# adaLN dots ordered behind the residual additions, second-GEMM weights requested two outputs ahead, norm tiles first, and mean squares of q and k token by token

## The chip, the core and the metric

The kernel is one program on one core of a Trainium2 chip. The metric is the device time of one execution in microseconds (us). Each version is timed by the median of several executions on the same chip; one more execution is recorded by the hardware profiler, and the profile and the trace come from that one. The engines have the names of the profile: PE (matmul; its weight loads are listed as PEld), DVE (vector), ACT (scalar and activation), POOL, and SP, which here only issues DMAs.

## What is computed

Two residual layers over x (512 tokens, 1024 features, fp32). Every layer modulates its norms by vectors computed from c:

```python
mod = silu(c) @ ada_w[layer] + ada_b[layer]          # 6 vectors of 1024
shift1, scale1, gate1, shift2, scale2, gate2 = split(mod)
h = rms_norm(x, norm_mix[layer]) * (1 + scale1) + shift1
y = mixer_conv_hgrn(h)          # layer 0
y = mixer_stick_breaking(h)     # layer 1: q, k = rms_norm of each head (64 wide), then attention
x = x + gate1 * y
h = rms_norm(x, norm_mlp[layer]) * (1 + scale2) + shift2
x = x + gate2 * (square(relu(h @ mlp_w1[layer])) @ mlp_w2[layer])   # 1024 -> 4096 -> 1024
```

## The kernel before

**Arithmetic.** Activations lie transposed: features on the 128 partitions, the 512 tokens along the free axis, in 8 tiles of features; tokens are often handled as two halves (hf 0 and 1) of 256. Every large matmul is done in three, with both operands split in a high and a low part: `mm3` issues whi x h_hi, whi x h_lo, wlo x h_hi (lines 281, 282, 283). A weight piece of 512 KB is loaded by SP into a raw buffer (`raw_w`; tile `wraw`, **3 buffers**, shared by both MLP matrices and the adaLN weights), cast to `whi` on ACT (L271) and reduced to `wlo` on DVE (L272), each with 4 buffers. The raw buffer is free for the next load when `wlo` is done.

**adaLN dots.** The modulation vectors are 1024-long dot products. `background(n)` takes the next n from a list: each loads a 512 KB piece of `ada_w` into a raw buffer and reduces it on DVE (`ada_dot`, L419; in the listings of order it is the row `ISA wraw,modr<-wraw,cb`, with a short second row `ISA modr`). 48 dots are spread over the four blocks of layer 0's MLP by the table `PIECES` (13, 13, 12 and 10 of them); in layer 1 the list is empty.

**The MLP** of layer 0 runs from about 264 to 604 us, that of layer 1 from 890 us to the end. It has a head (first norm half and four hidden tiles) and then four blocks b = 0 to 3. In each block a first GEMM makes hidden tiles in pairs (`pair`: seven 128x256 products from three sums of weights and activations, tiles `wa`, `wb`, `wc`, `wd`; `kept` copies one result to SBUF on ACT), the last step of which is deferred (`rest`), ending in a relu, square and split (`hidh`, `hidl` L291). The second GEMM then makes 8 outputs o (24 matmuls each, `products`): outputs 0 and 1 run their first seven eighths before and after `rest`, then both are finished, and o = 2 to 7 follow. `second(o)` asks for the weights w_o, `done(o)` adds the result to the residual (`x_add`, L505, tile `x`) and calls `background`. In block 3 `done` also squares x for the next norm (`nsq` on ACT L485, `nss` on DVE L490), only outputs 0 to 4 go this way, and 5, 6 and 7 follow in halves. While output 6 runs, `pair_w` asks for the weights of the next block's first pair.

**What sets the order.** PE's order in the MLPs is the order in which the code is written. DVE, ACT and SP are put in order in the MLP by the Tile scheduler, with priorities from the order of writing. The attention of layer 1 and both of its norms (the attention's, about 604 to 622 us, and the one before its MLP, about 884 to 898 us) are ordered by a planner (`on_pe`, `on_dve`, `on_act` give each operation's tiles, cost and a priority; lower goes first). Within an engine everything runs strictly in order.

**Two small places.** In `mlp_head` a timer `later(TN, ...)` with TN = 2.0 places the two matmuls with `ones` that finish the second half's norm (L496) after two of the eight k steps on PE. In attention, `mean_squares` sums the squares of q and k per head: a matmul with the 128x32 head selector `hs` (a slice of the tile `cons`) as the stationary operand and all the tokens moving (L1459), an ACT copy into `rows` (L1461), and one transpose per 128 tokens (L1465) to bring tokens onto partitions; DVE adds EPS (L1468).

Of the kernel before, what the change touches and what calls it, by code (L numbers as in the profile page):

```python
# [23 lines left out]
P = 128  # L24
T = 512
# [195 lines left out]
def trunk(tc, x_d, c_d, rep_d, small_d, const_d, ada_d, ws_d, win_d, wv_d, woab_d, w1_d, w2_d, wqk_d, wvc_d, woc_d, out_d):  # L221
# [130 lines left out]
    def acc():  # L352
        return mps.tile([P, T], F32, name="acc", tag="acc", bufs=4)
# [83 lines left out]
    def mcol(l, v, f):  # L437
        c = l * 48 + v * 8 + f
        return modc[:, c:c + 1]
# [62 lines left out]


    def x_add(o, ps, sl, l, v):
        dve.scalar_tensor_tensor(x[o][:, sl], ps, mcol(l, v, o), x[o][:, sl], op0=ALU.mult, op1=ALU.add)  # L505

# [174 lines left out]
    def later(delay, fn):  # L681
        count[0] += 1
        heapq.heappush(heap, (clk[0] + delay, count[0], fn))
# [458 lines left out]
    def mlp(l, last, hp, head, th, more=()):  # L1142

        nrm = Norm(1, 0, (7,)) if not last else None
        ahead = None
        for b in range(4):
            hid, rest = list(head) if b == 0 else [], lambda: None
            if b == 0:
                for n, j in enumerate((4, 5)):
                    whole_tile(more[n] if more else load_w(w1_d[l, j]), j, hp, hid)  # L1150
            for i in range(len(hid) // 2, 4):
                rest = pair(4 * b + i, hp, th, hid, rest, ahead or pair_w(l, 4 * b + i, hp))
                ahead = None
            n = 8 if b < 3 else 7 if last else 5
            second = lambda o: (acc(), load_w(w2_d[l, b // 2, o, b % 2], None, AT256 if o == n - 1 else AT512))

            def products(p, k0, k1):
                for k in range(k0, k1):
                    mm3(p[0], p[1], ks(k), hid[k], FULL, k == 0, k == 7)

            def done(o, ps):
                x_add(o, ps, FULL, l, GATE2)
                if b == 3:
                    if last:
                        sync.dma_start(out_d[o], x[o])
                    else:
                        nrm.add(o, FULL)
                if o < len(PIECES[b]):
                    background(PIECES[b][o])

            p0 = second(0)
            products(p0, 0, 7)
            rest()
            p1 = second(1)
            products(p1, 0, 7)
            for o, p in enumerate((p0, p1)):
                products(p, 7, 8)
                done(o, p[0])
            for o in range(2, n):
                p = p1 if o == n - 1 and b < 3 else second(o)  # L1180
                if o == n - 2 and b < 3:

                    p1, ahead = second(n - 1), pair_w(l, 4 * b + 4, hp)
                    next(ahead)
                    next(ahead)
                products(p, 0, 8)
                done(o, p[0])
                if o == n - 2 and b < 3:
                    w = next(ahead)
                    ahead = [w]  # L1190
# [109 lines left out]
    rows_ = in_ap([P, T], F32, "rows")  # L1300
# [99 lines left out]
    def finish(parts, hf, l, which, table, after=()):  # L1400
# [12 lines left out]
        for i in range(NT):  # L1413
            t_, g, sh = tth[i][hf], l * 16 + which * 8 + i, mcol(l, SHIFT1 if which == 0 else SHIFT2, i)
            hi, lo = hh[hf][i]

            on_dve(310, lambda i=i, t_=t_, g=g: dve.scalar_tensor_tensor(t_.t[:, sl], x[i][:, sl], gsc[:, g:g + 1], y.t,
                   op0=ALU.mult, op1=ALU.mult), (xh[i, hf], y), (t_,), -hf)
            on_act(256, lambda t_=t_, sh=sh, hi=hi: act.activation(hi.t[:, sl], t_.t[:, sl], AF.Identity, bias=sh), (t_,), (hi,), -hf,  # L1419
                   column=True)  # L1420
            on_dve(310, lambda t_=t_, sh=sh, hi=hi, lo=lo: dve.scalar_tensor_tensor(lo.t[:, sl], t_.t[:, sl], sh,  # L1421
                   hi.t[:, sl].bitcast(F32), op0=ALU.add, op1=ALU.subtract), (t_, hi), (lo,), -hf)


    QQ, KK, kraw, sqs, rq, oT, vs = {}, {}, {}, {}, {}, {}, {}
# [18 lines left out]
    def k_evict(p, ps, cut, sl):  # L1444
# [4 lines left out]
        on_act(n, lambda: act.copy(kraw[p].t[:, sl], cut(ps.t)), (ps,), (kraw[p],), 0, psum=True)  # L1449
        on_act(n, lambda: act.activation(sq.t[:, sl], cut(ps.t), AF.Square), (ps,), (sq,), 0, psum=True)  # L1450

    def mean_squares(p, bs, s0):

        if bs[0] == 0:
            rq[p] = [rrs[i].new() for i in range(4)]
        ms, row, col, m = miscs.new(), rows_.new(), miscs.new(), rq[p][0]
        sl, n = slice(P * bs[0], P * bs[-1] + P), P * len(bs)
        for s in range(2):
            on_pe(0.13, lambda s=s, sq=sqs[p, s, s0]: pe.matmul(ms.t[64 + 32 * s:96 + 32 * s, sl], hs, sq.t[:, sl], start=True, stop=True),  # L1459
                  (sqs[p, s, s0],), (ms,), 0)  # L1460
        on_act(n, lambda: act.copy(row.t[64:, sl], ms.t[64:, sl]), (ms,), (row,), 0, psum=True)  # L1461

        def flip():
            for b in bs:
                pe.transpose(col.t[:, 64 * b:64 * b + 64], row.t[64:, ks(b)], ident[64:, 64:])  # L1465
        on_pe(0.08 * len(bs), flip, (row,), (col,), 0)
        bb = slice(bs[0], bs[-1] + 1)
        on_dve(16, lambda: dve.tensor_scalar(  # L1468
            m.t.rearrange("p (s b h) -> p s b h", s=2, b=4)[:, :, bb],
            col.t[:, 0:256].rearrange("p (b s h r) -> p s b h r", b=4, s=2, h=2)[:, :, bb, :, 0], EPS, None, op0=ALU.add), (col,), (m,), 1)  # L1470

    def qk_norm(p):

# [332 lines left out]
```

## Time and profile before

| | before |
|---|---|
| median of 3 runs | 1236.03 us (1234.88 to 1237.93) |
| the profiled execution, its own time | 1238.95 us |
| its span | 1237.2 us, granted clock 0.997 |
| PE busy | 1213.8 us (98%) |
| DVE busy | 889.8 us (72%) |
| ACT busy | 618.5 us (50%) |
| DMA | 163.49 MB, mean 132 GB/s |

The profiled execution is 2.9 us above the median of the runs shown; 1.75 us of its time lie outside the span. An engine's busy time is a mean over very different stages. PE is the engine that is nearly always busy, so what moves the end is time in which PE waits, PE work added or removed, and stretches in which its granted clock is below 1.

### The profile page before, as it was taken

The page shows a single profiled execution, that of the slowest core. Times are in us where ns is not written, and L with a number is a line of the kernel's source. Part 1 is how long each engine was busy: PE and PEld are TensorE (multiplying, and loading weights), DVE is VectorE, ACT ScalarE, POOL GpSimd, SP SyncE. Part 2 cuts the span into 40 slices and gives each one's busy share as a digit, 9 for nine tenths or more (in the row PEclk, how much of TensorE's full clock was granted, in tenths as well). Part 3 has the DMA queues.
Part 4 walks back from the last instruction along what each step waited for, and adds up shares of the span by engine and source line. Part 5 has one row for each costly group of instructions (what it writes and reads, how often), then busy time and mean ns, then how long its engine had stood idle before and what let it go on. Part 6 is the DMA issues. An engine that isn't in the chain of part 4 may idle for free.

```text
span 1237.2 us, 19078 instructions
## 1 busy us (share of the span) xinstructions
PE 1213.8 (98%) x7601; PEld 1054.9 (85%) x7601; DVE 889.8 (72%) x1433; ACT 618.5 (50%) x1111; POOL 11.2 (1%) x24
## 2 busy tenths in 40 slices
PE   7999999999999999999999999999999999999998
PEld 6888877889799898898977778777898898998997
DVE  7996868779688787787867773669785585665752
ACT  4333232347257265274558754668464283472650
POOL 0000000000000000000200000000000000000000
PEclk9999999999999999999999999999999999999999
DMA  8765443623745726627432212322114223143141
GB/s 294 252 215 167 152 155 126 209 75 103 242 134 171 259 98 211 215 87 246 145 102 69 69 51 88 100 69 86 52 35 137 85 103 124 57 143 102 54 152 51
DMA packets 46329, 163.49 MB, mean 132 GB/s; under 512 B 5264, under 2 KB 5784, under 8 KB 46240
## 3 DMA queue, kind: packets, MB, share of 16 engines
q1 hardware_dynamic: 46096, 161.78, 39.4%
q8 instruction: 59, 0.97, 0.3%
q10 hardware_dynamic: 144, 0.49, 0.1%
q14 instruction: 30, 0.25, 0.1%
HBM read 155.96 MB, written 2.10 MB: 128 GB/s over the span
## 4 chain that ended last, share of the span: by engine, by line
PE 77%; DVE 10%; DMA 7%; ACT 4%; issue 2%; SPq 0%; ACTq 0%; DVEq 0%
PE b L281 19%; PE b L282 19%; PE b L283 19%; DMA wraw<-in_ada 2%; DMA raw<-in_ws 2%; DVE wlo L272 2%; PE acc L281 2%; PE acc L282 2%; PE acc L283 2%; PE b L1539 2%; PE b L1560 1%; DMA wraw<-in_w 1%; PE b L1595 1%; ACT whi L271 1%; PE b L1459 1%
## 5 line engine op out<-in xcount | busy, mean ns | idle before, releaser
L271 ACT CAST whi<-wraw 128x1024 fp32r<-128x1024 f32 x123 | 128.1, 1048 | 225.1 <-PE b L282 86.2
L282 PE MATMUL b<-hidl,whi 128*128 128x512 f32 (+1 forms) x544 | 205.8, 378 | 2.1 <-DVE hidl L291 2.1
L281 PE MATMUL b<-hidh,whi 128*128 128x512 f32 (+1 forms) x544 | 205.5, 378 | 0.0
L283 PE MATMUL b<-hidh,wlo 128*128 128x512 f32 (+1 forms) x544 | 205.1, 377 | 0.0
L281 PE MATMUL b<-hh,whi 128*128 128x256 f32 (+1 forms) x632 | 196.1, 310 | 1.5 <-ACT hh L1419 1.5
L282 PE MATMUL b<-hl,whi 128*128 128x256 f32 (+1 forms) x632 | 192.0, 304 | 0.7 <-DVE hl L1421 0.7
L283 PE MATMUL b<-hh,wlo 128*128 128x256 f32 (+1 forms) x632 | 192.0, 304 | 0.0
L272 DVE TENSOR_TENSOR wlo<-wraw,whi 128x1024 fp32r<-128x1024 f32 x123 | 150.0, 1223 | 57.1 <-ACT whi L271 55.6
L281 PEld LDWEIGHTS b<-hh,whi 128*128 128x128 f32 x632 | 119.6, 189 | 13.5 <-issue 7.2
L282 PEld LDWEIGHTS b<-hl,whi 128*128 128x128 f32 x632 | 120.7, 191 | 5.4 <-DVE hl L1421 1.1
L283 PEld LDWEIGHTS b<-hh,wlo 128*128 128x128 f32 x632 | 119.4, 189 | 5.3
L282 PEld LDWEIGHTS b<-hidl,whi 128*128 128x128 f32 x544 | 102.4, 188 | 22.3 <-DVE hidl L291 3.8
L505 DVE SCALAR_TENSOR_TENSOR x<-b,modc,x 128x512 f32<-128x512 f32 (+1 forms) x100 | 67.7, 684 | 74.4 <-PE b L283 74.2
L283 PEld LDWEIGHTS b<-hidh,wlo 128*128 128x128 f32 x544 | 102.2, 188 | 19.2 <-DVE wlo L272 0.2
L281 PEld LDWEIGHTS b<-hidh,whi 128*128 128x128 f32 x544 | 102.1, 188 | 18.7
L419 DVE CUSTOM_DVE_ANT_0 wraw<-wraw,cb 128x1024 f32<-128x1024 f32 x80 | 97.2, 1222 | 23.1 <-DMA wraw<-in_ada 22.8
L272 DVE TENSOR_TENSOR wlo<-tt,whi 128x1024 fp32r<-128x1024 f32 x52 | 63.4, 1221 | 26.0 <-ACT whi L271 25.4
L271 ACT CAST whi<-tt 128x1024 fp32r<-128x1024 f32 x52 | 53.4, 1050 | 42.5 <-PE b L282 27.7
L1372 DVE TENSOR_TENSOR wlo<-raw,whi 128x1024 fp32r<-128x1024 f32 x36 | 44.0, 1222 | 24.8 <-ACT whi L1371 24.6
L291 DVE TENSOR_TENSOR hidl<-cm,hidh 128x256 fp32r<-128x256 f32 (+1 forms) x90 | 44.6, 512 | 20.6 <-ACT hidh L290 19.5
L281 PE MATMUL acc<-hh,whi 128*128 128x512 f32 x128 | 52.2, 408 | 0.0
L1523 DVE TENSOR_TENSOR_SCAN om<-om,pat 128x772 f32<-128x772 f32 (+2 forms) x24 | 46.5, 1937 | 5.8 <-ACT om L1519 5.8
(378 smaller groups left out, 2634.5 us busy)
## 6 DMA issues: line engine op xcount, KB each, us to landing
wraw<-in_w SPq DMA_DIRECT2D x122, 512.0 KB, 4.0
wraw<-in_ada SPq DMA_DIRECT2D x80, 512.0 KB, 3.9
eraw<-in_ada SPq DMA_DIRECT2D x16, 512.0 KB, 3.7
wraw<-in_win SPq DMA_DIRECT2D x16, 512.0 KB, 3.4
raw<-in_wqk SPq DMA_DIRECT2D x16, 512.0 KB, 4.0
raw<-in_ws SPq DMA_DIRECT2D x8, 512.0 KB, 6.1
wraw<-in_woab SPq DMA_DIRECT2D x8, 512.0 KB, 3.2
raw<-in_wvc SPq DMA_DIRECT2D x8, 512.0 KB, 3.2
```

The costliest lines, as they stand in the source:

```text
L271: act.copy(hi, raw)
L272: dve.tensor_tensor(lo, raw, hi.bitcast(F32), op=ALU.subtract)
L281: pe.matmul(ps, whi, h[0][:, hs], start=start, stop=False, **kw)
L282: pe.matmul(ps, whi, h[1][:, hs], start=False, stop=False, **kw)
L283: pe.matmul(ps, wlo, h[0][:, hs], start=False, stop=stop, **kw)
L291: dve.tensor_tensor(lo[:, sl], t_[:, sl], hi[:, sl].bitcast(F32), op=ALU.subtract)
L419: dve.tensor_tensor_reduce(out=raw, in0=raw, in1=cb, scale=1.0, scalar=0.0, op0=ALU.mult, op1=ALU.add, accum_out=modr[:, col:col + 1])
L505: dve.scalar_tensor_tensor(x[o][:, sl], ps, mcol(l, v, o), x[o][:, sl], op0=ALU.mult, op1=ALU.add)
L1372: on_dve(1024, lambda: dve.tensor_tensor(lo.t, raw.t, hi.t.bitcast(F32), op=ALU.subtract), (raw, hi), (lo,), 1)
L1459: on_pe(0.13, lambda s=s, sq=sqs[p, s, s0]: pe.matmul(ms.t[64 + 32 * s:96 + 32 * s, sl], hs, sq.t[:, sl], start=True, stop=True), (sqs[p, ...
L1523: on_dve(2 * nw, lambda: dve.tensor_tensor_scan(s_(), s_(), pats[i][:, ::-1], 0.0, op0=ALU.mult, op1=ALU.max), (om,), (om,), 2)
L1539: pe.transpose(tp.t[:, o_:o_ + P], be.t[:, w0:w0 + P], ident)
```

## The change

Four edits.

1. In the MLP, `done(o)` now asks for the weights of output o + 2 itself, ahead of `background`, and the dots that `background` issues are tied behind the addition to x of that output by an ordering edge on DVE (`tc.issue_after`, no instruction and no semaphore). The loads of the dots are not tied.
2. In the head of layer 0's MLP the timer goes from TN to 2 TN.
3. In layer 1's norms the first three tiles of the first half get priority -1.
4. `mean_squares` takes the squares as the stationary operand, 128 tokens at a time, and two columns of `hs` as the moving one, so that tokens come out on partitions: 8 matmuls per call for 512 tokens, and neither ACT copy nor transposes; the tile `rows` is gone.

```diff
-            def done(o, ps):
-                x_add(o, ps, FULL, l, GATE2)
+            def done(o):
+                added = x_add(o, ps_[o][0], FULL, l, GATE2)
                 if b == 3:
                     if last:
                         sync.dma_start(out_d[o], x[o])
                     else:
                         nrm.add(o, FULL)
+                if o + 2 < n:
+                    ps_[o + 2] = second(o + 2)
                 if o < len(PIECES[b]):
-                    background(PIECES[b][o])
-            p0 = second(0)
-            products(p0, 0, 7)
+                    with tc.issue_after(added.ins):
+                        background(PIECES[b][o])
+            ps_ = {0: second(0)}
+            products(ps_[0], 0, 7)
             rest()
-            p1 = second(1)
-            products(p1, 0, 7)
-            for o, p in enumerate((p0, p1)):
-                products(p, 7, 8)
-                done(o, p[0])
+            ps_[1] = second(1)
+            products(ps_[1], 0, 7)
+            for o in range(2):
+                products(ps_[o], 7, 8)
+                done(o)
             for o in range(2, n):
-                p = p1 if o == n - 1 and b < 3 else second(o)
                 if o == n - 2 and b < 3:
-                    p1, ahead = second(n - 1), pair_w(l, 4 * b + 4, hp)
+                    ahead = pair_w(l, 4 * b + 4, hp)
...
     def mlp_head(l, nin, hp):
-        later(TN, lambda: nin.finish(acc(256), 1))
+        later(2 * TN, lambda: nin.finish(acc(256), 1))
...
+            first = -1 if hf or i < 3 else 0
             on_dve(310, lambda ...: ..., (xh[i, hf], y), (t_,), -hf)   # all three: -hf becomes first
...
+    hs2 = hs[:, 0:32:16]
     def mean_squares(p, bs, s0):
-        for s in range(2):
-            on_pe(0.13, lambda s=s, sq=sqs[p, s, s0]: pe.matmul(ms.t[64 + 32 * s:96 + 32 * s, sl], hs, sq.t[:, sl], start=True, stop=True),
-                  (sqs[p, s, s0],), (ms,), 0)
-        on_act(n, lambda: act.copy(row.t[64:, sl], ms.t[64:, sl]), (ms,), (row,), 0, psum=True)
-        def flip():
-            for b in bs:
-                pe.transpose(col.t[:, 64 * b:64 * b + 64], row.t[64:, ks(b)], ident[64:, 64:])
-        on_pe(0.08 * len(bs), flip, (row,), (col,), 0)
+        def sums_of():
+            for s in range(2):
+                for b in bs:
+                    pe.matmul(col.t[:, 8 * s + 2 * b:8 * s + 2 * b + 2], sq[s].t[:, ks(b)], hs2, start=True, stop=True)
+        on_pe(0.22 * len(bs), sums_of, sq, (col,), 0)
```

DVE at block 0's second GEMM, before. `wlo` is the split of a weight piece, `hidl` the split of a hidden tile that PE reads, x_61 and x_62 the residual tiles of outputs 0 and 1.

```order
L272 TENSOR_TENSOR wlo<-wraw,whi 128x1024
L291 TENSOR_TENSOR hidl<-cm,hidh 128x256
L419 ISA wraw,modr<-wraw,cb 128x1024
L419 ISA modr 128x1
L419 ISA wraw,modr<-wraw,cb 128x1024
L419 ISA modr 128x1
L419 ISA wraw,modr<-wraw,cb 128x1024
L419 ISA modr 128x1
L505 SCALAR_TENSOR_TENSOR x_61<-b_2826,modc,x_61 128x512
L505 SCALAR_TENSOR_TENSOR x_62<-b_2870,modc,x_62 128x512
L432 TENSOR_TENSOR gsc<-modr,adb 128x8
L272 TENSOR_TENSOR wlo<-wraw,whi 128x1024
```

Eight of the block's 13 dots stand ahead of the first two additions there, the last three of them in these rows. The same place in the changed kernel:

```order
L272 TENSOR_TENSOR wlo<-wraw,whi 128x1024
L291 TENSOR_TENSOR hidl<-cm,hidh 128x512
L291 TENSOR_TENSOR hidl<-cm,hidh 128x256 x2
L505 SCALAR_TENSOR_TENSOR x_61<-b_2826,modc,x_61 128x512
L505 SCALAR_TENSOR_TENSOR x_62<-b_2870,modc,x_62 128x512
L419 ISA wraw,modr<-wraw,cb 128x1024
L419 ISA modr 128x1
L419 ISA wraw,modr<-wraw,cb 128x1024
L419 ISA modr 128x1
L272 TENSOR_TENSOR wlo<-wraw,whi 128x1024
L505 SCALAR_TENSOR_TENSOR x_63<-b_2902,modc,x_63 128x512
```

The hidden tiles' splits have no dot among them any more, and all 13 dots of the block stand behind the addition of output 1 (x_62): a1 and a2, the split of w4, the addition of output 2, and then, further down, a3 a4 a5, x3, w5, a6 a7, x4, a8, w6, a9 a10, x5, a11, w7, a12 a13, x6, and only then the next pair's `wa` and sums. (a1 to a13 are the dots, x2 to x6 the additions, w4 to w7 the splits of those outputs' weights.) In blocks 1 and 2 it is the same, with 13 and 12 dots.

ACT at the end of block 3, before. Outputs 5, 6 and 7 use the last `whi` casts of `wraw`; `raw` holds weights of attention; x_65 is the residual tile of output 4, L339 an activation table load.

```order
L271 CAST whi<-wraw 128x1024
L485 ACTIVATE nsq<-x_63 128x512
L271 CAST whi<-wraw 128x1024 x2
L485 ACTIVATE nsq<-x_64 128x512
L271 CAST whi<-wraw 128x1024
L1371 CAST whi<-raw 128x1024 x2
L485 ACTIVATE nsq<-x_65 128x512
L339 ACT_TABLE_LOAD
```

And in the changed kernel:

```order
L485 ACTIVATE nsq<-x_64 128x512
L485 ACTIVATE nsq<-x_65 128x512
L339 ACT_TABLE_LOAD
L271 CAST whi<-wraw 128x1024 x3
L1372 CAST whi<-raw 128x1024 x3
```

The casts of w5, w6 and w7 stand behind the square of output 4 and behind the table load; SP likewise issues eight dot loads in a row ahead of w5, w6, w7.

DVE at the norm before layer 1's MLP, before (x_66 to x_68 are the last residual tiles of attention, `tt` the normed tiles of the first half, `hl` their low parts, which PE reads):

```order
L505 SCALAR_TENSOR_TENSOR x_65<-b_8687,modc,x_65 128x256
L505 SCALAR_TENSOR_TENSOR x_66<-b_8700,modc,x_66 128x256
L1395 TENSOR_TENSOR nss<-nss,nsq 128x256
L505 SCALAR_TENSOR_TENSOR x_67<-b_8713,modc,x_67 128x256
L1395 TENSOR_TENSOR nss<-nss,nsq 128x256
L505 SCALAR_TENSOR_TENSOR x_68<-b_8727,modc,x_68 128x256
L1417 SCALAR_TENSOR_TENSOR tt<-x_61,gsc,ny 128x256
```

And in the changed kernel:

```order
L505 SCALAR_TENSOR_TENSOR x_65<-b_8669,modc,x_65 128x256
L1419 SCALAR_TENSOR_TENSOR tt<-x_61,gsc,ny 128x256
L1419 SCALAR_TENSOR_TENSOR tt<-x_62,gsc,ny 128x256
L1419 SCALAR_TENSOR_TENSOR tt<-x_63,gsc,ny 128x256
L1396 TENSOR_TENSOR nss<-nss,nsq 128x256
L1423 SCALAR_TENSOR_TENSOR hl_8735<-tt,modc,hh_8723 128x256
```

Three normed tiles and their low parts now stand ahead of the last three additions of the other half. On PE the planner puts the whole of attention in another order as a result of edits 3 and 4; the two `ones` matmuls of edit 2 stand 24 matmuls later.

More of the change, by code (lines that the diff above doesn't have):

```diff
@@ L504, in x_add @@
     def x_add(o, ps, sl, l, v):
-        dve.scalar_tensor_tensor(x[o][:, sl], ps, mcol(l, v, o), x[o][:, sl], op0=ALU.mult, op1=ALU.add)
+        return dve.scalar_tensor_tensor(x[o][:, sl], ps, mcol(l, v, o), x[o][:, sl], op0=ALU.mult, op1=ALU.add)
     new_h()
@@ L1167, in done @@
                         nrm.add(o, FULL)
+                if o + 2 < n:
+                    ps_[o + 2] = second(o + 2)
                 if o < len(PIECES[b]):
-                    background(PIECES[b][o])
-            p0 = second(0)
-            products(p0, 0, 7)
+                    with tc.issue_after(added.ins):
+                        background(PIECES[b][o])
+            ps_ = {0: second(0)}
+            products(ps_[0], 0, 7)
             rest()
-            p1 = second(1)
-            products(p1, 0, 7)
-            for o, p in enumerate((p0, p1)):
-                products(p, 7, 8)
-                done(o, p[0])
+            ps_[1] = second(1)
[3 more added lines that the diff above has]
+                done(o)
             for o in range(2, n):
-                p = p1 if o == n - 1 and b < 3 else second(o)
                 if o == n - 2 and b < 3:
-                    p1, ahead = second(n - 1), pair_w(l, 4 * b + 4, hp)
+                    ahead = pair_w(l, 4 * b + 4, hp)
                     next(ahead)
                     next(ahead)
-                products(p, 0, 8)
-                done(o, p[0])
+                products(ps_[o], 0, 8)
+                done(o)
                 if o == n - 2 and b < 3:
-                    w = next(ahead)
-                    ahead = [w]
+                    ahead = [next(ahead)]
         if not last:
@@ L1299, in trunk @@
     vrs, oTs, krows = in_ap([P, 4, 256], F32, "v", 2), in_ap([P, T], F32R, "oT", 10), in_ap([4, T], F32R, "krow")
-    rows_ = in_ap([P, T], F32, "rows")
     rrs = [in_ap([P, 16], F32, f"r{i}", n) for i, n in enumerate((2, 1, 3, 3))]
@@ L1415, in finish @@
             hi, lo = hh[hf][i]
+            first = -1 if hf or i < 3 else 0
             on_dve(310, lambda i=i, t_=t_, g=g: dve.scalar_tensor_tensor(t_.t[:, sl], x[i][:, sl], gsc[:, g:g + 1], y.t,
-                   op0=ALU.mult, op1=ALU.mult), (xh[i, hf], y), (t_,), -hf)
-            on_act(256, lambda t_=t_, sh=sh, hi=hi: act.activation(hi.t[:, sl], t_.t[:, sl], AF.Identity, bias=sh), (t_,), (hi,), -hf,
+                   op0=ALU.mult, op1=ALU.mult), (xh[i, hf], y), (t_,), first)
+            on_act(256, lambda t_=t_, sh=sh, hi=hi: act.activation(hi.t[:, sl], t_.t[:, sl], AF.Identity, bias=sh), (t_,), (hi,), first,
                    column=True)
             on_dve(310, lambda t_=t_, sh=sh, hi=hi, lo=lo: dve.scalar_tensor_tensor(lo.t[:, sl], t_.t[:, sl], sh,
-                   hi.t[:, sl].bitcast(F32), op0=ALU.add, op1=ALU.subtract), (t_, hi), (lo,), -hf)
+                   hi.t[:, sl].bitcast(F32), op0=ALU.add, op1=ALU.subtract), (t_, hi), (lo,), first)
     QQ, KK, kraw, sqs, rq, oT, vs = {}, {}, {}, {}, {}, {}, {}
@@ L1455, in mean_squares @@
             rq[p] = [rrs[i].new() for i in range(4)]
-        ms, row, col, m = miscs.new(), rows_.new(), miscs.new(), rq[p][0]
-        sl, n = slice(P * bs[0], P * bs[-1] + P), P * len(bs)
-        for s in range(2):
-            on_pe(0.13, lambda s=s, sq=sqs[p, s, s0]: pe.matmul(ms.t[64 + 32 * s:96 + 32 * s, sl], hs, sq.t[:, sl], start=True, stop=True),
-                  (sqs[p, s, s0],), (ms,), 0)
-        on_act(n, lambda: act.copy(row.t[64:, sl], ms.t[64:, sl]), (ms,), (row,), 0, psum=True)
-        def flip():
-            for b in bs:
-                pe.transpose(col.t[:, 64 * b:64 * b + 64], row.t[64:, ks(b)], ident[64:, 64:])
-        on_pe(0.08 * len(bs), flip, (row,), (col,), 0)
+        col, m, sq = miscs.new(), rq[p][0], [sqs[p, s, s0] for s in range(2)]
+        view = lambda t_: t_.rearrange("p (s b h) -> p s b h", s=2, b=4)
+        def sums_of():
[3 more added lines that the diff above has]
+        on_pe(0.22 * len(bs), sums_of, sq, (col,), 0)
         bb = slice(bs[0], bs[-1] + 1)
-        on_dve(16, lambda: dve.tensor_scalar(
-            m.t.rearrange("p (s b h) -> p s b h", s=2, b=4)[:, :, bb],
-            col.t[:, 0:256].rearrange("p (b s h r) -> p s b h r", b=4, s=2, h=2)[:, :, bb, :, 0], EPS, None, op0=ALU.add), (col,), (m,), 1)
+        on_dve(16, lambda: dve.tensor_scalar(view(m.t)[:, :, bb], view(col.t[:, 0:16])[:, :, bb], EPS, None, op0=ALU.add), (col,), (m,), 1)
     def qk_norm(p):
```

## Prediction

> **What bounds the kernel now.** I read the engine totals and the chain first: they say which engine's time is the program's time.
>
> ```profile
> span 1237.2 us, 19078 instructions
> PE 1213.8 (98%) x7601; PEld 1054.9 (85%) x7601; DVE 889.8 (72%) x1433; ACT 618.5 (50%) x1111; POOL 11.2 (1%) x24
> PE 77%; DVE 10%; DMA 7%; ACT 4%; issue 2%; SPq 0%; ACTq 0%; DVEq 0%
> ```
>
> PE is busy in all but 23 us. So three things move the end: a PE wait removed, a PE wait added, and PE work. The waits of PE come next; the rows that the change touches are these.
>
> ```profile
> PE b L496 <- DVE nss L490: 2.4, 1, 2.4
> PE b L282 <- DVE hidl L291: 2.1, 4, 1.1
> PE b L281 <- ACT hh L1419: 1.5, 1, 1.5
> PE b L282 <- DVE hl L1421: 0.7, 1, 0.7
> ```
>
> All that the removal of waits can bring is 6.7 us. The third view is the timeline of DVE and PE over block 0's second GEMM, since the dots move there (start and length in us, engine, line, operation, tiles, and in brackets the idle time before it and what ended it).
>
> ```profile
> 313.83 1.23 DVE L419 CUSTOM_DVE_ANT_0 wraw<-wraw,cb 128x1024 f32<-128x1024 f32 x1 [1.73 <-DMA wraw<-in_ada]
> 314.98 1.02 DVE L291 TENSOR_TENSOR hidl<-cm,hidh 128x512 fp32r<-128x512 f32 x2
> ...
> 320.66 1.22 DVE L272 TENSOR_TENSOR wlo<-wraw,whi 128x1024 fp32r<-128x1024 f32 x1 [2.37 <-ACT whi L271]
> ...
> 322.17 1.22 DVE L419 CUSTOM_DVE_ANT_0 wraw<-wraw,cb 128x1024 f32<-128x1024 f32 x1
> 323.32 1.22 DVE L419 CUSTOM_DVE_ANT_0 wraw<-wraw,cb 128x1024 f32<-128x1024 f32 x1
> 325.25 1.22 DVE L419 CUSTOM_DVE_ANT_0 wraw<-wraw,cb 128x1024 f32<-128x1024 f32 x1 [0.71 <-DMA wraw<-in_ada]
> 326.41 1.41 DVE L505 SCALAR_TENSOR_TENSOR x<-b,modc,x 128x512 f32<-128x512 f32 x2
> 329.05 1.23 DVE L272 TENSOR_TENSOR wlo<-wraw,whi 128x1024 fp32r<-128x1024 f32 x1 [1.17 <-ACT whi L271]
> 337.39 1.23 DVE L272 TENSOR_TENSOR wlo<-wraw,whi 128x1024 fp32r<-128x1024 f32 x1 [2.44 <-ACT whi L271]
> 345.54 1.22 DVE L272 TENSOR_TENSOR wlo<-wraw,whi 128x1024 fp32r<-128x1024 f32 x1 [1.24 <-ACT whi L271]
> 349.08 0.69 DVE L1071 TENSOR_TENSOR tt<-wraw 128x512 f32<-128x512 f32 x1
> 351.05 0.40 PE L281 MATMUL b<-hidh,whi 128*128 128x512 f32 x1
> 356.65 0.28 PE L281 MATMUL b<-hh,whi 128*128 128x256 f32 x1
> 357.60 0.28 PE L283 MATMUL b<-hh,wlo 128*128 128x256 f32 x1
> wraw<-in_ada SPq DMA_DIRECT2D x12, 512.0 KB, 4.6
> wraw<-in_w SPq DMA_DIRECT2D x9, 512.0 KB, 4.4
> wraw<-in_win SPq DMA_DIRECT2D x16, 512.0 KB, 3.4
> ```
>
> (The first two DMA rows are those of 300 to 350 us, the last is the whole program's row for another weight.) What the reader is to see: DVE, though busy, waits here for weight pieces. From one `wlo` (320.66) to the next (329.05, 337.39) it is 8.4 us, for four pieces, a w and three dots: 2.1 us a piece. Three raw buffers, each held 4.5 us by its load and 1.2 to 2.5 us by its use, give just about that. The last weight, w7, is split at 345.54 to 346.8 and PE needs it at 351.05 + 0.45 (third matmul of output 7). So the block has 4.7 us in hand at w7, for 13 dots of which eight are done ahead of 326.41.
>
> **Edit 1, the dots and the weights.** Removed: the dots between the hidden tiles' splits, so the wait on `hidl` goes: gain 2.1, of which 1.1 in block 0 (taken as that). All PE times of block 0 below are therefore 1.1 earlier than in the rows.
>
> Added: no instruction, but an order. Output 2 starts 5 x 5.45 us (24 x 0.227) ahead of output 7, at 349.95 - 27.25 = 322.7, so the additions of outputs 0 and 1 end at about 322.7 + 0.2 + 0.7 = 323.6. Until then DVE may touch no dot, the three buffers stand full (a1, a2, w4), and SP, which waits for a buffer at a3, has everything else queued behind it: a4, a5, w5 and on. What is queued on DVE behind the waiting addition is every later `wlo`. From 323.6 on I go through it by hand: a1 to 324.8, a2 to 325.9, w4 to 327.1; a3 is issued when a1 ends and lands 3.4 later, done at 329.4. Then the listed order holds eleven pieces up to w7 (a4 a5 w5 a6 a7 a8 w6 a9 a10 a11 w7). At 2.1 each that is 352.5; buffer by buffer with 4.4 for a load, 1.2 for a dot and 2.4 for cast plus split it is 351.7. w7 is needed at 350.4: late 1.3 to 2.1. The next pair comes behind it. Its first raw piece is issued when w7's split ends, lands 4.4 later, is cast (1.05) and split (1.2): +6.7; then three sums of 0.6 on DVE, the next cast and its split: +10.8 to 10.95, so `wb` is whole at 362.5 to 363.4. PE needs it after the first product (12 x 0.119 = 1.4) and two matmuls, at 355.55 + 1.4 + 0.25 = 357.2. Late 5.3 to 6.2 in all; the 1.3 to 2.1 are part of it. In the profile the second sum stands at 349.08, so this chain is early today and sets nothing. Block 1 has the same 13 dots: the same. Block 2 has one dot fewer after w5: 2 less, 3.3 to 4.2. Block 3 ends otherwise, and needs rows of its own.
>
> ```profile
> 593.63 1.05 ACT L1371 CAST whi<-raw 128x1024 fp32r<-128x1024 f32 x1 [1.50 <-DMA raw<-in_wqk]
> 596.95 0.63 ACT L485 ACTIVATE nsq<-x 128x512 f32<-128x512 f32 x1
> 597.59 1.28 ACT L339 ACT_TABLE_LOAD   x1
> 358.27 0.37 ACT L1098 COPY kept<-b 128x256 f32<-128x256 f32 x1 [0.55 <-PE b L283]
> ```
>
> There ACT is strictly in order: output 4's end on PE, its addition (0.2 + 0.75), its square 0.63, the table load 1.28, and only then the cast of w5, 1.05: output 5 starts 4.0 late at the least. Its load can be issued only after a8's dot, and its split stands behind a9 and a10 on DVE: by the same walk 5 to 6.4. In blocks 0 and 1 there is a floor of the same kind: ACT now has the copy `kept` of the first product ahead of the cast for `wb`, so copy, cast and split (0.2 + 0.37 + 1.05 + 1.0) follow the product: 2.65 late even with weights on time.
>
> Bounds: if a load took 3.4 (the nearest row below), a piece would cost (3.4 + 1.2) / 3 = 1.55 for a dot and 2.0 for a w, 1.65 in the mean; eleven pieces are 5 us shorter and only the floors stay: 2.65 + 2.65 + 1.1 + 4.0 = 10.4. At the top of each range it is 6.2 + 6.2 + 4.2 + 6.4 = 23, a little more if the loads of all blocks crowd. I take the walk, which uses the DMA rows of this very window: **loss 20**. Asking for w_o+2 earlier costs nothing and brings nothing by itself: whi and wlo have four buffers, and SP's order of requests differs from before by one or two places only.
>
> **Edit 2.** The 2.4 us wait for `nss` is covered by 24 matmuls of 0.115 = 2.8 us. The second half's tiles come no earlier while PE reaches them 2.6 sooner; a part may come back there. Gain 2.0 (0.5 to 2.6).
>
> **Edit 3.** The head of layer 1's MLP has these rows.
>
> ```profile
> 890.71 0.28 PE L283 MATMUL b<-oT,stq 128*128 128x256 f32 x1
> 892.49 0.38 PE L281 MATMUL b<-hh,whi 128*128 128x256 f32 x1 [1.51 <-ACT hh L1419]
> 893.54 0.58 PE L282 MATMUL b<-hl,whi 128*128 128x256 f32 x1 [0.66 <-DVE hl L1421]
> 896.69 0.28 PE L281 MATMUL b<-hh,whi 128*128 128x256 f32 x1
> 891.42 1.66 DVE L1417 SCALAR_TENSOR_TENSOR tt<-x,gsc,ny 128x256 f32<-128x256 f32 x4
> 893.27:896.69 3.42, 3.15 (x15) 3.15 (x15) 3.42 (x10) 1.96 (x5) 0.00 (x0) 0.50 0.00 0
> 267.26:269.97 2.71, 0.28 (x4) 0.08 (x2) 2.50 (x7) 1.52 (x4) 0.00 (x0) 1.00 0.00 0
> ```
>
> PE waits 1.5 + 0.7 and then runs 15 matmuls at a granted clock of 0.50, 0.21 us apart where 0.115 is usual: 1.4 us more. Moved ahead of three additions and two sums of 0.4, the first `tt` starts some 1.8 us sooner; the low part then needs three tiles and one sum ahead, not four tiles. I take a wait of 0.5 left and no half clock: gain 3.0 (2 to 3.6).
>
> **Edit 4.** The groups of the summing, and the nearest group with 128 columns of weights and few moving ones:
>
> ```profile
> L1459 PE MATMUL b<-nsq,cons 128*32 128x512 f32 x24 | 12.5, 605 | 0.0
> L1459 PE MATMUL b<-nsq,cons 128*32 128x256 f32 x16 | 4.6, 391 | 1.8 <-ACT nsq L1450 1.8
> L1465 PE MATMUL b<-cons,rows 64*128 64x64 f32 x32 | 4.1, 238 | 0.0
> L807 PE MATMUL lv<-Qt,Kt 128*128 128x64 f32 x48 | 5.8, 273 | 0.6 <-DVE Kt L838 0.6
> ```
>
> 21.2 us go. What comes is 8 pairs x 8 matmuls with two records each, as fp32 has in these rows: 128 records at 5.8 / 48 = 0.121 us, 15.5. That is 5.7 less, and ten visits of PE to a short job fewer, some 0.1 each; the planner's other order of attention may take or give 3. [...] ACT's copies and DVE's wait lie beside PE work. Gain 5.5 (2 to 6.5).
>
> **Sum.** Losses 20; gains 2.1 + 2.0 + 3.0 + 5.5 = 12.6; net +7.4 on 1238.95. The profiled execution stands 2.9 above the median shown, so the median goes from 1236.03 to 1243.4; with half a microsecond for a chance of the clock below, **1244 us**, slower. A change of 0.3% (3.7 us) is about what a measurement of this kernel can tell from none.
>
> **Rivals.** (a) The other side: pieces come at 1.65 us once the buffers are released, since the DMA then has nothing else to carry. Then the loss is 10.4, and with edits 2 to 4 at the better part of their ranges (2.6 + 3.4 + 6.5 + 2.1 = 14.6) the time is 1232. It decides at a loss of about 9 to 10, or 1.65 us a piece; the 8.4 us for four, seen twice in a row, speak against it; the DMA rate of 3.4 us loads speaks for it. (b) Halfway, 13 lost and 13 won: 1236, no change. (c) The clock: in blocks 0, 1 and 3 PE would stand for 3 to 5 us at a time. After 2.2 us of waits at 890 the clock was 0.50 for 3.42 us; after 2.4 us at 267 it stayed at 1.00. If each of four stalls cost such a spell, 3.42 us at half speed, 1.7 lost, it is 6.8 more: 1251. [...] (d) The tie does nothing, the dots running where they ran: excluded by the order.
>
> **How the numbers follow.** Forecast 0.60 (alone 1240 to 1249); (a) 0.12; (b) 0.14; (c) 0.14. Slower by over 0.3%: nearly all of the forecast and (c), 0.72; within: (b), and edges of (a) and the forecast, 0.17; faster: most of (a), 0.11. The range from 1232 to 1253 takes in (a)'s time and (c)'s, and leaves out the tails of both.
>
> **What would show it.** In the trace after: no PE wait on `hidl` in layer 0's MLP and none of over 0.5 on `nss` at 267; the first dots of blocks 0 to 2 right behind two additions, then a piece every 2.1 us; PE waits on `wlo` or `whi` of output 7 and of `wb` of together 5 to 6 in blocks 0 and 1, 3 to 4 in block 2, and 4 to 6 ahead of output 5 in block 3; the `nsq` matmuls at 0.12 apart; no 0.50 clock after 890. I am wrong if pieces come below 1.7 us apart, if PE's waits in blocks 0 to 3 sum to under 10, or if attention grows by its new order.

## The result, and the profile after

The changed kernel takes **1255.8 us** (median; 1254.2 to 1258.1), the kernel before 1237.0 in the runs beside it: ratio 1.0155, 95% interval 1.0132 to 1.0178, slower by 18.8 us. The forecast was slower, 1244, with a range to 1253. The sign and the places of the loss were right; the forecast had less than half of its size, and the result lies 2.8 us above the range.

From the page of the changed kernel, the span, PE's total and the row of slices for PE's clock; the last row is the clock of the kernel before:

```profile
span 1256.3 us, 19194 instructions
PE 1218.6 (97%) x7657; PEld 1073.0 (85%) x7657; DVE 891.0 (71%) x1433; ACT 612.0 (49%) x1101; POOL 12.9 (1%) x24
PEclk9999999999989999989889999999999999999999
PEclk9999999999999999999999999999999999999999
```

PE's busy time rose by 4.8 us although edit 4 took matmul work away. The clock row says where to look: four of its slices (of 31.4 us each) are below 9, three in layer 0's MLP and one, from 628 to 660 us, that reaches into attention; the kernel before has none.

PE's waits over the whole run, the longest rows:

```profile
PE b L281 <- ACT whi L271: 14.6, 7, 5.8
PE b L283 <- DVE wlo L272: 5.2, 10, 0.8
```

The rows for `nss` L490 (2.4) and for `hh` (1.5) are gone, that for `hidl` went from 2.1 to 0.2. New are 19.8 us of waiting on the two halves of the split weights, where there had been 0.3.

Both kernels by stage, from PE's first matmul of a stage to that of the next (columns as in the prediction: us, busy time of PE, PEld, DVE, ACT, POOL, then the granted clock, DMA share, GB/s). Before: the head and the pairs of the first block, then the second GEMM of block 0, the pairs behind it, the second GEMMs of blocks 1 and 2 (the pairs behind each take 38.16 us again), block 3, attention, layer 1's MLP.

```profile
264.65:310.11 45.46, 43.03 (x318) 40.84 (x317) 41.24 (x77) 31.15 (x63) 0.00 (x0) 1.00 0.23 74
310.11:356.65 46.54, 45.43 (x206) 37.39 (x205) 33.64 (x51) 13.45 (x19) 0.00 (x0) 1.00 0.70 234
356.65:394.81 38.16, 38.16 (x325) 38.16 (x324) 31.76 (x49) 27.85 (x54) 0.00 (x0) 1.00 0.31 102
394.81:440.40 45.59, 45.42 (x207) 37.27 (x205) 35.61 (x54) 13.95 (x19) 0.00 (x0) 1.00 0.74 250
478.56:524.51 45.95, 45.38 (x206) 37.34 (x205) 33.85 (x52) 14.10 (x19) 0.00 (x0) 1.00 0.69 233
562.67:609.86 47.19, 46.93 (x282) 41.59 (x281) 36.16 (x60) 22.44 (x35) 0.08 (x1) 1.00 0.68 227
609.86:892.49 282.63, 277.11 (x1862) 222.67 (x1860) 194.24 (x325) 179.92 (x362) 9.64 (x15) 1.00 0.25 75
892.49:1233.90 341.41, 340.47 (x2132) 308.00 (x2132) 208.97 (x308) 164.81 (x294) 0.00 (x0) 1.00 0.28 94
```

The same stages after, with the pairs behind blocks 1 and 2 in rows of their own:

```profile
263.61:307.02 43.41, 42.36 (x318) 39.96 (x317) 39.83 (x74) 31.28 (x63) 0.00 (x0) 1.00 0.19 59
307.02:357.59 50.57, 47.76 (x206) 38.25 (x205) 30.03 (x46) 10.84 (x16) 0.00 (x0) 0.97 0.63 210
357.59:398.83 41.24, 38.97 (x326) 38.56 (x324) 35.93 (x56) 30.71 (x56) 0.00 (x0) 0.96 0.34 116
398.83:447.55 48.72, 45.97 (x207) 37.15 (x205) 30.04 (x47) 10.33 (x15) 0.00 (x0) 1.00 0.65 210
447.55:489.06 41.51, 38.93 (x325) 38.32 (x324) 37.08 (x56) 31.83 (x58) 0.00 (x0) 1.00 0.37 124
489.06:535.58 46.52, 45.83 (x207) 37.23 (x206) 28.37 (x44) 9.73 (x15) 0.00 (x0) 1.00 0.63 205
535.58:579.86 44.28, 41.74 (x325) 41.04 (x324) 37.16 (x56) 31.65 (x58) 0.00 (x0) 0.92 0.35 119
579.86:635.58 55.72, 49.47 (x282) 43.85 (x281) 37.43 (x62) 21.07 (x34) 0.06 (x1) 0.91 0.61 197
635.58:913.84 278.26, 271.44 (x1918) 235.32 (x1917) 192.04 (x321) 174.32 (x350) 11.36 (x15) 0.99 0.25 76
913.84:1253.00 339.16, 338.64 (x2134) 306.28 (x2132) 210.94 (x313) 164.86 (x296) 0.00 (x0) 1.00 0.29 95
```

The head is 2.0 us shorter. Block 0 with the pairs behind it is 7.1 longer, block 1 6.5, block 2 6.7 and block 3 8.5, together 28.8. Attention is 4.4 shorter, layer 1's MLP 2.2, and the part ahead of the first row, which the change does not touch, 1.0. All together that is +19.1, the difference of the spans. Within the 28.8, PE's waits explain 20.5 (with the rest of `hidl` and 0.5 on `hidh`), of which 2.1 had been there before. The clock column explains the rest: (1 - clock) x length sums to 11.7, and since PE stood still for part of the half-clock time anyway, about 10 of it are lost.

Windows of 1 us show the half clock (0.50) more exactly: 23.9 us of it in blocks 0, 2 and 3, 19.5 of them with PE at work, so 9.8 us lost; and 6.8 us in attention (652.1 to 659.0), with PE at work, so 3.4 lost. The kernel before has none in either place. Without the latter, attention would have been some 7.8 us shorter.

DVE in block 0, where the prediction's walk began, and the waits of PE that came of it in blocks 0 and 3:

```profile
320.10 1.43 DVE L505 SCALAR_TENSOR_TENSOR x<-b,modc,x 128x512 f32<-128x512 f32 x2 [3.74 <-PE b L283]
321.44 1.22 DVE L419 CUSTOM_DVE_ANT_0 wraw<-wraw,cb 128x1024 f32<-128x1024 f32 x1
...
323.73 1.22 DVE L272 TENSOR_TENSOR wlo<-wraw,whi 128x1024 fp32r<-128x1024 f32 x1
...
333.57 1.23 DVE L272 TENSOR_TENSOR wlo<-wraw,whi 128x1024 fp32r<-128x1024 f32 x1 [1.16 <-ACT whi L271]
341.41 1.23 DVE L272 TENSOR_TENSOR wlo<-wraw,whi 128x1024 fp32r<-128x1024 f32 x1 [1.56 <-ACT whi L271]
349.53 1.23 DVE L272 TENSOR_TENSOR wlo<-wraw,whi 128x1024 fp32r<-128x1024 f32 x1 [1.44 <-ACT whi L271]
349.55 0.50 PE L281 MATMUL b<-hidh,whi 128*128 128x512 f32 x1 [1.58 <-ACT whi L271]
360.72 0.39 PE L281 MATMUL b<-t0h,whi 128*128 128x256 f32 x1 [1.51 <-ACT whi L271]
361.99 0.58 PE L283 MATMUL b<-t0h,wlo 128*128 128x256 f32 x1 [0.76 <-DVE wlo L272]
614.63 0.58 PE L281 MATMUL b<-hidh,whi 128*128 128x256 f32 x1 [5.79 <-ACT whi L271]
```

DVE stands still 3.7 us ahead of the additions while the three buffers are full (the two dots and w4 behind the additions follow without a wait for data). The dots begin behind the additions. From the split of w4 (323.73) to that of w7 (349.53) twelve pieces take 25.8 us, 2.15 a piece; the last eight of them, from w5 (333.57) to w6 (341.41) to w7, take 7.8 and 8.1, 2.0 a piece. PE then waits for w7 (1.6), for the next pair's second weight (1.5 and 0.8) and, in block 3, 5.8 ahead of output 5. Behind each of these waits it runs at 0.50 for a while (351.8 to 355.2, 362.0 to 365.4, 611.2 to 621.4).

### The profile page after: what moved, and what is told of

Its sections match the earlier page's. It is cut to its first block, busy times and chain, and to the rows that moved or that the text cites. A ratio compares the mean times of both kernels' runs of the same rounds, so it can differ in the third digit from the quotient of the medians.

```text
span 1256.3 us, 19194 instructions
## 1 busy us (share of the span) xinstructions
PE 1218.6 (97%) x7657; PEld 1073.0 (85%) x7657; DVE 891.0 (71%) x1433; ACT 612.0 (49%) x1101; POOL 12.9 (1%) x24
## 4 chain that ended last, share of the span: by engine, by line
PE 72%; DVE 14%; DMA 7%; ACT 3%; issue 3%; SPq 0%; ACTq 0%; DVEq 0%
PE b L283 17%; PE b L281 17%; PE b L282 16%; DMA wraw<-in_w 5%; PE acc L281 4%; PE acc L282 3%; PE acc L283 3%; DVE wlo L272 2%; DVE wraw L419 2%; DMA wraw<-in_ada 1%; DVE om L1523 1%; DVE eraw L419 1%; PE b L1560 1%; ACT whi L271 1%; PE b L1539 1%
## 5 line engine op out<-in xcount | busy, mean ns | idle before, releaser
L281 PE MATMUL b<-hidh,whi 128*128 128x512 f32 (+1 forms) x544 | 207.9, 382 | 10.2 <-ACT whi L271 9.7
L282 PE MATMUL acc<-hl,whi 128*128 128x512 f32 x128 | 49.9, 390 | 0.0
```

Of the source, the lines that this page charges most:

```text
L281: pe.matmul(ps, whi, h[0][:, hs], start=start, stop=False, **kw)
L282: pe.matmul(ps, whi, h[1][:, hs], start=False, stop=False, **kw)
```

## The experiments

Each was timed beside the kernel before on the same chip; the ratios are to that.

**1. The changed kernel without the tie.**

```diff
-                    with tc.issue_after(added.ins):
-                        background(PIECES[b][o])
+                    background(PIECES[b][o])
```

> The changed kernel without the tie: the dots may again stand ahead of the additions on DVE; weights asked for two outputs ahead and edits 2 to 4 stay. Theory (the tie makes the weights late, and the long waits bring half-clock spells): no PE wait over 1 us on whi or wlo in layer 0's MLP, no half clock there, and 1237 - 2.0 (edit 2) - 6.6 (edits 3 and 4, as the two traces differ) = 1228 us (1225 to 1232). Rival (the requests two ahead push the dots' loads back in SP's queue and make the weights late by themselves): 1245 or more.

1231.99 us, ratio 0.9958 (0.9942 to 0.9974), 4.9 faster than before. In layer 0's MLP no wait on `whi` is left; the longest left is 1.2 on `hidl`, `wlo` has 0.7, and there is no half clock. The tie causes the loss, 23.8 us; the rival falls. The time lies at the upper end of what was expected.

**2. The tie, with the requests where they were.**

```diff
-                if o + 2 < n:
-                    ps_[o + 2] = second(o + 2)
+            # w_o requested just ahead of output o's matmuls, as before
```

> Edits 2 to 4 and the tie, but the weights are requested where they were before. Theory (tie): the MLP of layer 0 stays 28 us longer than before, 1253 to 1258 us. Rival (requests two ahead): 1228 us.

1324.72 us, ratio 1.0698 (1.0673 to 1.0724): neither theory expected it. PE's longest row of waits, and DVE around output 3 of block 0:

```profile
PE b L281 <- ACT whi L271: 68.6, 12, 6.5
331.81 1.23 DVE L272 TENSOR_TENSOR wlo<-wraw,whi 128x1024 fp32r<-128x1024 f32 x1 [2.26 <-ACT whi L271]
340.26 0.75 DVE L505 SCALAR_TENSOR_TENSOR x<-b,modc,x 128x512 f32<-128x512 f32 x1 [7.23 <-PE b L283]
```

SP's order has w3 behind a3 a4 a5, so its load needs the buffer of a dot, and that dot is tied behind the addition of output 2. The load of w3 therefore starts only after output 2 is finished, and its load, cast and split (6.5 us) stand in the open; in the same way those of w4 and w5, and so in the other blocks, twelve waits in all, ten of them over 6 us. Against the same kernel without the tie (experiment 3) that is 93 us: 70.6 of waits on the split weights and, by windows on the trace, some 22 for 45 us of PE's work at half clock. The requests two ahead take each weight past one group of dots. So they are worth 69 us once the tie is there, and nothing without it (next).

**3. Edits 2 to 4 alone.**

> Edits 2, 3 and 4 alone, with the MLP loop of before. Both theories: 1228 us (1225 to 1232), that is 5 to 12 us faster than before. If edit 1 also had a gain of its own (the hidl waits, 2.1 us), this one is 1 to 2 us above the kernel without the tie.

1231.37 us, ratio 0.9945 (0.9927 to 0.9963). The same as without the tie (1231.99): requests two ahead alone bring nothing that can be measured, as predicted. Both medians are slower than the 1228 that the traces' stages promised. The clock may be the reason: of the five runs here, the two with a mean granted clock of 0.999 took 1227.8 and 1229.0 us, the three with 0.993 or 0.994 took 1231.4 to 1232.2, and the trace of experiment 1 has 10.2 us of half clock in attention.

**4. Edit 1 alone**, on the kernel before.

> The tie and the requests two ahead alone, everything else as before. Theory: the loss of layer 0's MLP is a thing of its own, 28.8 us in the traces: 1262 to 1268 us, with the same waits on whi and wlo (about 20 us) and half-clock spells. If part of the loss comes of edits 2 to 4 (PE arriving 2 us earlier, another phase of the clock), under 1260.

1265.96 us, ratio 1.0223 (1.0203 to 1.0244): 29.1 us lost by edit 1 by itself, with 14.6 on `whi` and 6.0 on `wlo`, and granted clocks of 0.986 to 0.989 in its four runs (0.994 to 0.999 for the kernel before). The loss does not need the other edits.

**5. Four raw buffers** in the changed kernel.

```diff
-        raw = wp.tile([P, 1024], F32, name="wraw", tag="raw", bufs=3)
+        raw = wp.tile([P, 1024], F32, name="wraw", tag="raw", bufs=4)
```

(and the same number at the other uses of the tag.)

> The changed kernel with four raw buffers in place of three (everywhere; the scheduler and the planner then order other parts a little otherwise too). Theory (after the tie the pieces come at the pace of three buffers): a piece every (4.4 + 1.2 to 2.4) / 4 = 1.4 to 1.7 us instead of 2.0, PE's waits on whi and wlo in layer 0's MLP fall from 20 us to the floors, 5 to 11, fewer half-clock spells: 1234 to 1244 us. Rival (the DMA's rate is the limit: 512 KB each 2.0 us is 260 GB/s): 2.0 us stays and the time is over 1250 us.

1240.01 us, ratio 1.0011 (0.9996 to 1.0026). The waits of PE from 255 to 640 us, of which the second row belongs to attention, and the rows of the first and last of the twelve pieces from w4 to w7 of block 0:

```profile
PE b L281 <- ACT whi L271: 4.1, 1, 4.1
PE b L1467 <- ACT nsq L1452: 2.0, 1, 2.0
PE b L283 <- DVE wlo L272: 2.0, 4, 0.7
324.11 1.22 DVE L272 TENSOR_TENSOR wlo<-wraw,whi 128x1024 fp32r<-128x1024 f32 x1
345.43 1.23 DVE L272 TENSOR_TENSOR wlo<-wraw,whi 128x1024 fp32r<-128x1024 f32 x1 [0.40 <-ACT whi L271]
```

With one buffer more the twelve pieces take 21.3 us, 1.78 each instead of 2.15, and blocks 0 to 2 have no wait on `whi` left. The 4.1 is the one ahead of output 5 of block 3, which the prediction gave as 4.0 at the least, for the table load and the cast on ACT. The pace of three buffers is the cause in blocks 0 to 2, not the DMA's rate: the same loads came faster here. Block 3 keeps its loss: the 4.1, and 6.8 us of half clock behind it. Against experiment 12, which is this kernel without edit 1, the time is still 9.8 us longer, and the two traces, which are 4.9 apart, do not account for all of that.

**6. Dots without their loads.**

```diff
-            ada_piece(l, v, f)                       # load, then reduce raw * cb
+            raw = wp.tile(..., tag="raw", bufs=3)    # no load
+            dve.tensor_tensor_reduce(out=raw, in0=cb, in1=cb, ..., accum_out=modr[:, col:col + 1])
```

> The changed kernel, the 48 dots of layer 0's MLP without their loads: each still takes a raw buffer and its 1.2 us of DVE behind the same additions, but reads the resident vector twice (so the modulation values are not the reference's). Theory (the loads' pace): PE's waits on whi and wlo under 8 us, mostly at the floors of ACT's order: 1230 to 1240 us. Rival (DVE's own time, 13 dots behind the addition, is too long): over 1250 us.

1235.44 us, ratio 0.9982 (0.9973 to 0.9991), with these waits on the split weights in layer 0's MLP:

```profile
PE b L281 <- ACT whi L271: 4.0, 1, 4.0
PE b L283 <- DVE wlo L272: 1.1, 2, 0.7
```

The dots' 1.2 us each on DVE behind the additions do no harm that shows here; their loads in the shared buffers do. Again block 3's 4.0 is the only wait on `whi` left.

**7. Work in PE's waits.**

```diff
+        for _ in range(fill):      # 16, first pair of blocks 1 to 3
+            pe.matmul(c, wa[0][:, ks(0)], hT[0][0][:, H[0]], start=True, stop=True)
         prod(c, wb, 0, t1, True)
...
+                    for _ in range(46):      # ahead of output 5 of block 3
+                        pe.matmul(ps[o, hf], w_f[:, ks(0)], hid[0][0][:, H[0]], start=True, stop=True)
```

> The changed kernel with work for PE where it waits longest, into a bank that the next matmul overwrites: 46 matmuls of 256 columns (5.3 us) ahead of output 5 of block 3, 16 (1.9 us) ahead of the second product of the first pair of blocks 1 to 3 of layer 0: 11 us of PE work more. Theory (the waits bring the half clock): the work lies in the waits, the half-clock spells behind them go, 1246 to 1251 us. Rival (the half clock comes of something else, or the waits are not where they are read): 1256 to 1267 us.

1253.39 us, ratio 1.0127 (1.0112 to 1.0142): with 11 us more of matmuls it takes 2.4 us less than the changed kernel, hardly more than the noise (the intervals overlap). The time lies between those of the theory and of the rival, so by itself it decides nothing. The extra work was hidden, but the clock was not 1.00 yet. Half clock in blocks 0 to 3 fell from 23.9 to 10.2 us; the last waits, such as 1.4 and 0.8 left ahead of output 5, still had it behind them:

```profile
534.65:577.33 42.68, 41.92 (x340) 41.72 (x341) 37.77 (x56) 31.64 (x58) 0.00 (x0) 0.96 0.34 114
577.33:633.09 55.76, 53.63 (x329) 48.24 (x327) 37.45 (x62) 21.22 (x34) 0.07 (x1) 0.97 0.61 197
```

**8. All long waits filled**: as 7, with 9, 11 and 4 matmuls of 512 columns ahead of output 7 of blocks 0 to 2, 22 in the pairs, 58 ahead of output 5.

> As the kernel with filled waits, but all of the long ones filled: 9, 11 and 4 matmuls of 512 columns ahead of output 7 of blocks 0 to 2, 22 of 256 ahead of the second product of the next pair, 58 of 256 ahead of output 5 of block 3: 5.5 + 7.6 + 6.7 = 19.8 us of PE work more, as much as PE waited on whi and wlo there. Theory (the waits bring the half clock, and with PE kept at work it stays at 1.00): the work costs nothing and the spells go, some 8 us: 1246 to 1250 us, granted clock of 0.99 to 1.00 in every block of layer 0's MLP. Rival (the half clock has another cause): 1255 us or more, windows of 0.9 to 0.97 as in the changed kernel.

1258.36 us, ratio 1.0164 (1.0139 to 1.0189). The clock did what the theory said in the profiled execution: it is 1.00 in each of the seven stages of blocks 0 to 3. Two of them:

```profile
536.38:578.45 42.07, 40.36 (x348) 39.56 (x346) 37.21 (x56) 30.79 (x58) 0.00 (x0) 1.00 0.33 117
578.45:632.75 54.30, 53.40 (x341) 47.88 (x339) 37.45 (x62) 21.48 (x34) 0.07 (x1) 1.00 0.62 203
```

The time did not; by time alone the rival has it. I had sized the fill for all of the waits, and it overshot some, with new waits behind it (2.6 us on `kept`). The stages tell the two apart: in the changed kernel blocks 0 to 3 take 328.6 us (307.02 to 635.58), 20.5 of them waits, so 308.1 beside them; here they take 324.8 (307.95 to 632.75), 19.8 of them fill and some 7 to 8 waits, so 297 to 298; in the kernel before, 299.75 less 2.1, 297.6. The 10 us by which the changed kernel exceeds both are what its half clock costs. The profiled execution here, at 1255.0 us and a mean clock of 0.997, was the fastest of four; the others had 0.993, 0.993 and 0.996 and took up to 1260.1. So the median does not show the 10 us, only the stages of one execution do, and where the other three lost their time is not on record.

**9 to 11. Edits 2, 3 and 4, each alone**, on the kernel before.

> Edit 2 alone (the timer). By the stage of the two traces it is worth 2.0 us: 1235 us (1234 to 1236.5). Rival (given back later): 1237, no change.

1239.53 us, ratio 1.0018 (1.0003 to 1.0033): no gain. The wait at the head is gone, and that on `hidl` is down to 0.2 as well, but PE, 1.4 us earlier at block 0's second GEMM (308.67 against 310.11), finds the weight of output 5 late, by 1.3 and then 0.5 us. PE's timeline:

```profile
338.81 0.50 PE L281 MATMUL b<-hidh,whi 128*128 128x512 f32 x1 [1.32 <-ACT whi L271]
```

> Edit 3 alone (norm tiles first). Wait and half clock at the head of layer 1's MLP go: 2 to 3.6 us, 1233 to 1235 us, unless the planner's other order of attention costs as much: 1237.

1234.30 us, ratio 0.9973 (0.9962 to 0.9983): 3.4 us, as expected.

> Edit 4 alone (mean squares token by token). 21 us of PE work become 16 (128 records of 0.124 in the changed kernel's trace): 1231 to 1233 us. Rival (attention's own waits and the planner's order set its length, not PE's work): within 1.5 us of 1237.

1231.47 us, ratio 0.9950 (0.9933 to 0.9968): 6.2 us, as expected.

**12. Edits 2 to 4 with four raw buffers**, as a version to keep.

> Edits 2 to 4 without edit 1, with four raw buffers: the dots among the hidden tiles' splits then find their data landed. Theory: the remaining hidl waits go, 1228 to 1231 us. Rival (the loads crowd one another, or the mixer's and attention's other order costs): 1233 or more.

1230.24 us, ratio 0.9934 (0.9917 to 0.9950), the lowest median of all, 7.7 us below the kernel before; the `hidl` wait is down to 0.2. Against experiment 3 it is not clear of noise.

## Why the prediction was right in its places and wrong in its size

- **The loss by late weights** (taken as 20): right, at the low end of the walk or a little below it. 19.8 us of waits on `whi` and `wlo`, at the places named: output 7, the next pair's second weight, output 5 of block 3. By block they are 4.4, 5.3, 3.2 and 6.3, where the walk had 5.3 to 6.2 twice, 3.3 to 4.2 and 5 to 6.4. The walk's step of 2.1 us a piece measured 2.0 to 2.15; rival (a)'s 1.65 did not come. Experiments 1, 5 and 6 show the chain: tie, full buffers, pace of three buffers.
- **The clock** (half a microsecond in the sum; rival (c) with four spells, 6.8 us, at a chance of 0.14): this is the step that failed, a term of the sum that was far too small. Half-clock stretches followed the waits in blocks 0, 2 and 3, seven spells of 3.4 us where rival (c) had four, and cost about 10 us; two more in attention cost 3.4. Rival (c) was not an alternative to the forecast but a consequence of it: four blocks of long waits and an observed row of 0.50 behind waits of 2.2 us should have put several spells into the sum itself. The prediction's own two rows, where one wait of two (2.2 us at 890, not the 2.4 at 267) had half clock behind it, would have added 3.4 us to the sum, not 0.5. That the waits bring the half clock is shown by taking them away: in blocks 0 to 3 the traces have 23.9 us of it in the changed kernel, 10.2 with part of the waits filled (7), 0 with all of them filled (8), 6.8 in each of 5 and 6, all behind the wait of block 3, and 0 without the tie (1 and 3).
- **The floors.** That of block 3, 4.0, was right (4.1 and 4.0 in experiments 5 and 6). That of 2.65 in blocks 0 and 1, `kept` ahead of the cast for `wb` on ACT, was not there: with the weights on time PE had no such wait. The low end of the loss, 10.4, was therefore too high by about 5.
- **Requests two ahead** "bring nothing by themselves": right (1 against 3), but the prediction missed that they are what keeps the tie from costing 93 us (2 against 3).
- **`hidl`** (2.1): the wait went from 2.1 to 0.2, as said, but edit 1 is not needed for it: edit 2 alone has 0.2 too. **Edit 2** (2.0): the wait went, as in the head's 2.0 of the trace, but alone it is given back in block 0. **Edit 3** (3.0): 3.4 alone; one wait of 0.5 on `hl` left at the head (914.64) and no half clock there, as said. **Edit 4** (5.5): 6.2 alone. The 2 at the low end of its range was the author's estimate for dearer records, which no run shows; the runs showed 0.118 to 0.124 us a record. Its group of matmuls:

```profile
L1467 PE MATMUL b<-cons,nsq 128*128 128x2 f32 x128 | 15.9, 252 | 2.0 <-ACT nsq L1452 2.0
```

  That is 15.9 / 128 = 0.124 us a record where 0.121 was taken; eight of the records ran at half clock, and in experiments 3 and 11, where none did, it is 15.1 / 128 = 0.118.
- **The sum.** The gains, 12.6 there, come to 10.7 by stages of the trace (2.1 + 2.0 + 4.4 + 2.2), or 14.1 if the 3.4 that the half clock took in attention are counted with the clock. With waits 20.5, clock 13 and gains 14 the working gives +19 to +20; measured are 18.8. So losses by waiting and gains were forecast about right, and the whole miss of 11 us is the size of the clock. How many spells an execution gets was beyond the prediction: in the changed kernel's trace block 1, with 5.3 us of waits on the weights, had none, and block 2, with 3.2, had two (last section).

## What to carry to other kernels

A background task that shares a small ring of buffers with the critical loads must not be made to wait on the critical engine's results: while it waits it holds the ring, and what is behind it in the DMA queue comes at the pace of the ring, here 2.0 to 2.15 us a piece with three buffers. Before adding an ordering edge, count the buffers, go through the queue piece by piece, and ask what is held while the waiting instruction stands. And a forecast of PE waits should price the half clock with them: in the changed kernel's trace PE's waits for output 7 of block 0 (1.58 and 0.53) and for the next pair's second weight (1.51 and 0.76) had it behind them, the one ahead of output 5 of block 3 (5.79) ended in it, and the seven spells of 3.41 us in blocks 0 to 3 cost about 10 us.

## What the runs showed of the hardware

**When the clock fell.** In the trace of the changed kernel the stretches at half clock (0.50) behind the start-up begin at 351.76, 362.00, 539.50, 611.17 and 652.13 us and last 3.41, 3.41, 6.83, 10.24 and 6.83 us; their starts are 3, 52, 21 and 12 times 3.413 us apart. The kernel before has one, 3.41 us from 893.27 (in both a last one is cut off by the end of the program). The starts are not those of the waits: ahead of output 5 of block 3 PE stood from 608.84 to 614.63, and the clock fell 2.3 us into that, at 611.17; in block 0 it fell at 351.76, when PE was at work again. The rows below are steps of 3.41 us counted from such a start (length, then PE's busy time; the clock is the third number from the end). From the changed kernel:

```profile
348.35:351.76 3.41, 1.69 (x6) 1.11 (x7) 2.23 (x2) 1.04 (x1) 0.00 (x0) 1.00 0.71 226
351.76:355.18 3.42, 3.42 (x10) 2.64 (x9) 2.04 (x5) 0.00 (x0) 0.00 (x0) 0.50 0.82 256
437.10:440.51 3.41, 1.76 (x8) 1.13 (x6) 1.40 (x3) 0.56 (x1) 0.00 (x0) 1.00 0.83 279
440.51:443.93 3.42, 2.35 (x9) 1.65 (x10) 2.86 (x4) 0.49 (x1) 0.00 (x0) 1.00 0.65 186
```

And from the kernel before, around its two waits that the prediction compared (the stretch behind the last row is the one at 0.50 that it shows):

```profile
265.22:268.63 3.41, 2.32 (x21) 2.12 (x19) 3.41 (x10) 1.69 (x4) 0.00 (x0) 1.00 0.00 0
268.63:272.05 3.42, 2.08 (x14) 1.98 (x15) 1.13 (x3) 1.69 (x4) 0.00 (x0) 1.00 0.00 0
889.86:893.27 3.41, 1.51 (x11) 1.11 (x10) 3.41 (x10) 2.47 (x7) 0.00 (x0) 1.00 0.07 29
```

PE idle for 1.72 us of one row (348.35) is followed by 0.50 in the next. In block 1 much the same waits are split between two rows, 1.65 and 1.07 us idle (437.10 and 440.51), and the clock stays at 1.00. The wait of 2.4 us at 267 was cut into 1.09 and 1.34, and the clock stayed at 1.00; the two that come to 2.2 at 890 left 1.90 idle in one row, and behind it are 3.41 us at 0.50. The other four falls in the changed kernel's trace had 2.27 us (from 358.59), 1.97 (536.08), 2.32 (607.76) and 1.55 (648.72) of idle PE in the 3.41 us ahead of them. So 1.55 had a fall behind it and 1.65 had none, with the caution that the ends of matmuls are modelled; what decides is not shown. Equal executions differ too: the mean granted clock of the five runs of experiment 3 is 0.993 to 0.999.

**Few moving columns.** A matmul of two moving columns in fp32, with 128 columns of weights, took two records here, of 0.118 us each (experiments 3 and 11) or 0.124 in the mean (the changed kernel, eight records at half clock), as much a record as one with 64 moving columns in the kernel before (5.8 / 48 = 0.121): between these two, fewer columns saved nothing.
